# Output projection with seven block products instead of eight for the first 768 tokens

## The chip, the cores and the metric

The kernel runs on one core of a Trainium2 chip. The metric is the device time of one execution in microseconds (us). Three runs of the kernel before took 2946.74, 2948.99 and 2950.83 us; the median is 2948.99.

A core has five engines that run at their own pace and meet at semaphores: TensorE (PE, matmul; its weight loads are listed as PEld), VectorE (DVE), ScalarE (ACT), GpSimd (POOL) and SyncE (SP). SP here only issues DMAs; GpSimd and ScalarE issue DMAs too, beside their own work, and an engine does its instructions in the order in which they stand.

## What is computed

The reference is one layer of a decoder with two token mixers, a state space recurrence (S5) and gated linear attention (GLA). 1088 tokens go through it: 64 of eight short sequences (stored first) and 1024 of the prompt. What matters here is the end of the layer:

```python
merged = sigmoid(m_a) * a_out + sigmoid(m_b) * b_out
y = x + gate[:, None] * (merged @ w_out)          # w_out: 2048 x 2048
...
y_prompt = rms_norm(hp, final_norm_gain)          # the same for the samples
```

So `merged @ w_out` is a product of 1088 x 2048 by 2048 x 2048. After it come a gate per channel (for the samples per sequence and channel), the residual x, and a root mean square norm over the 2048 channels of each token.

## The kernel before

Channels lie on the 128 partitions and tokens along the free dimension, so an activation of 2048 channels is 16 tiles of [128, 1088]. A float32 operand is held in two parts, `hi` and `lo`, and `mm3` (lines 64 to 71) makes a product of them in three matmuls: hi with hi, hi with lo, lo with hi. The weights are split while they stream. `wsplit` (line 44) loads a [128, 512] quarter of a column tile on SP's queue into a raw buffer `wraw`, ScalarE rounds it to `whi` (line 54) and VectorE subtracts to get `wlo` (line 56). There are two raw buffers in the weight pool and, where a second pool is given, two more; `whi` and `wlo` have six buffers each.

The projection is `final` (lines 1058 to 1132). It goes over three token chunks, `FCH = [(0, 416), (416, 416), (832, 256)]`, and for each over 16 column tiles j and 16 k tiles, so 16 x 16 x 3 = 768 matmuls a chunk. In the first chunk the column tiles go in groups of six and three first, because the merged activations are loaded and split meanwhile:

```python
x = self.stage("mx")
nc.gpsimd.dma_start(x, self.mscr[k])
mg.append(self.split_act(x, True, nc.gpsimd if k % 3 == 1 else None))
```

`mscr` is the DRAM scratch into which `merge` (lines 1027 to 1055) writes the merged columns, one [128, 1088] tile per column tile. The 32 activation tiles of the pool `act` hold first the operands of the two merge products and then the 16 merged tiles in two parts.

For each finished column tile `ev` (line 1070) loads the residual on GpSimd's queue (line 1073), multiplies the sum in PSUM by the gate and adds the residual on VectorE (1081 to 1084), squares on ScalarE (1089), adds to the running sum of squares `acc` on VectorE (1090), and scales on ScalarE (1091). After 16 column tiles the root is taken (1126 to 1128), and y is multiplied by it and stored, two column tiles at a time (1130 to 1132), on VectorE and GpSimd:

```python
e, r = (nc.gpsimd, rc) if (i % 3 == 2 if last else i not in (0, 2)) else (V, rs)
e.tensor_tensor(ys[i], ys[i], r.unsqueeze(1).broadcast_to([P, 2, n]), mul)
```

The order on each engine is set when the kernel is built: a scheduler takes the instructions in the order in which the program writes them and lets an engine take a later one where, by its own model of the times, the earlier one is not ready or has no free buffer. On the chip each engine then keeps that order. Buffers of a pool with the same tag are used in rotation.

Of the kernel before, what the change touches and what calls it, by code (L numbers as in the profile page):

```python
# [26 lines left out]
FCH = [(0, 416), (416, 416), (832, 256)]  # L27
# [4 lines left out]
class Hybrid:  # L32
# [58 lines left out]
    def product_k(self, w, js, act, nk, evict):  # L91
        """Two or three column tiles side by side, in steps of 2 k tiles."""
# [9 lines left out]
        if shared:  # L102
            # opens a sum over the whole bank for the two that share it
# [25 lines left out]
    def rsqrt(self, out, v, tmp):  # L129
        """out = (v + eps) ** -0.5; v is read twice, tmp is a scratch tile."""  # L130
        nc = self.nc
        nc.scalar.activation(tmp, v, AF.Sqrt, bias=self.eps)
        nc.vector.reciprocal(out, tmp)
        self.newton(out, v, tmp)
# [9 lines left out]
    def setup(self):  # L144
# [13 lines left out]
        # four unit matrices of 32 rows above each other  # L158
# [24 lines left out]
    def ada_chunk(self, j, ps):  # L183
        """mod[:, 2j:2j+2, :]: 256 columns of silu(c) @ w_ada + b_ada, channels on partitions."""
# [12 lines left out]
    def ada_mm(self, ps, k0, raw, n):  # L197
        """Rows of w_ada against silu(c), four k tiles side by side in groups of 32 columns."""
# [5 lines left out]
    def ada_out(self, j, ps):  # L204
# [6 lines left out]
        # the four column groups together  # L211
# [3 lines left out]
    def norm_in(self):  # L215
        """1 / rms of the tokens, on all partitions"""
# [28 lines left out]
    def modulate(self, k):  # L245
        """h[k] in two parts."""
# [4 lines left out]
        # gain * (1 + scale)  # L251
# [4 lines left out]
        # prompt: h without the shift, then samples  # L256
# [14 lines left out]
    # The two halves of the partitions hold the real and imaginary parts of the 64 states of a group.  # L271
# [3 lines left out]
    def s5_setup(self):  # L275
# [10 lines left out]
        with ExitStack() as ctx:  # L286
# [21 lines left out]
            def exp(out, x, w):  # L308
                """exp(x) to the last bits: 2**k times a polynomial"""
# [23 lines left out]
            # sine and cosine: nearest quarter turn, rest below pi/4, polynomials  # L333
# [59 lines left out]
            # cf = (abar - 1) / lambda  # L393
# [29 lines left out]
    def s5_tables_a(self, u):  # L423
# [21 lines left out]
        def outer(out, pr, pi, n, x, y, op):  # L445
            """out[g, t, h] = pr[g, t] * x[g, h] (op) pi[g, t] * y[g, h]"""
# [12 lines left out]
    def s5_tables_b(self, u, tables):  # L459
# [21 lines left out]
        # powers of the rotation between chunks, by doubling  # L481
# [86 lines left out]
    def s5_run(self):  # L568
        """All of S5, in steps between other products."""
# [26 lines left out]
    def evict_u(self, j, c, t0, n, ps):  # L596
        """u in rows of [8 tokens of a chunk][136 chunks]"""
# [18 lines left out]
        # parts of ga: hi, lo, hi  # L616
# [32 lines left out]
    def evict_v(self, j0):  # L649
        """v with tokens on partitions: blocks of 128 tokens, the first of 64"""  # L650
        nc = self.nc

        def ev(j, c, t0, n, ps):
# [10 lines left out]
            if first:  # L664
                # the samples again in the layout of parts
# [17 lines left out]
    def gla_pool(self, ctx):  # L683
# [25 lines left out]
    def gla_load(self, hd, t0, n):  # L709
# [10 lines left out]
        if n == 64:  # L720
            # read as columns that nothing comes of
# [11 lines left out]
    def gla_run(self):  # L733
        """All of the GLA, in steps between other products."""
# [21 lines left out]
    def gla_unit(self, hd, t0, n, inputs, following):  # L756
        """head hd, tokens t0:t0+n; n = 256: two chunks of 128 of the prompt; n = 64: the samples"""
# [13 lines left out]
        # log gates (times 16) and their sums within the chunks  # L771
# [20 lines left out]
        # scores, [s, t], by halving: pairs across the middle of blocks of 2m tokens  # L792
        # in blocks of 32 tokens: scd[s, chunk, t of the same block]
# [16 lines left out]
        def decays(m):  # L810
            """queries and keys of the blocks, with the decays from and to the middle"""
# [41 lines left out]
        # decays from the start and to the end of the chunks  # L853
# [21 lines left out]
        if samp:  # L875
            # each row its part
# [79 lines left out]
    def ada_gates(self):  # L956
        """The last eight column chunks of the conditioning product, in steps between other products."""
# [11 lines left out]
    def split_act(self, x, on_act=False, engine=None):  # L969
        """The two parts of a [128, T] tile."""  # L970
# [87 lines left out]
    def final(self):  # L1058
# [5 lines left out]
        for t0, n in FCH:  # L1064
# [29 lines left out]
            for js in groups:  # L1094
# [12 lines left out]
                if start:  # L1107
                    self.p2ctx.close()
                    p3 = self.pool("p3")
# [176 lines left out]
```

## Time and profile before

| | |
|---|---|
| runs | 2946.74, 2948.99, 2950.83 us |
| profiled execution, span from first to last instruction | 2947.8 us |
| PE busy | 2890.1 us (98%) |
| DVE, ACT, POOL busy | 1344.5, 941.1, 263.4 us |
| output projection, first matmul to end of span | 2525.8 to 2947.8 us |
| granted TensorE clock, mean | 0.994 of 2.4 GHz |

The profile is of one execution; the page gives its span, and the median of the runs lies 1.2 us above it. Busy time is the time in which an engine had an instruction at work. Matmuls overlap in the engine, so the pace of a matmul is read from the distance of starts and not from its own duration. A view by windows gives for each stretch the busy time and the count of instructions of each engine, the granted clock, the share of time in which the DMA engines were busy, and what they moved.

### The profile page before, as it was taken

The numbers are of one execution on the slowest core, as the hardware profiler recorded it, in microseconds if no ns is written. First come the engines' busy times: TensorE is split into PE (matmuls) and PEld (weight loads), VectorE is DVE, ScalarE is ACT, GpSimd is POOL, SyncE is SP. The second block draws the span as 40 slices with busy tenths as digits, with TensorE's granted clock in tenths as the row PEclk, the third lists the DMA queues.
The fourth block names the chain that finished last, engine by engine and source line by source line (L and its number), as shares of the span: only waits on it lengthen the run. The fifth ranks groups of instructions, "written<-read, shape, count | busy, mean of one in ns | idle before, by whom it ended". The sixth has DMA issues, their size and how long they took to land.

```text
span 2947.8 us, 49487 instructions
## 1 busy us (share of the span) xinstructions
PE 2890.1 (98%) x19584; PEld 2762.2 (94%) x19584; DVE 1344.5 (46%) x3424; ACT 941.1 (32%) x1735; POOL 263.4 (9%) x430
## 2 busy tenths in 40 slices
PE   7999999999999999999999999999999999999988
PEld 3799999999989999999999999999999999899988
DVE  3587778751234444444453111114662233556455
ACT  4222222222234434443443111422232111444434
POOL 0002122210000000000000000301010000203021
PEclk9999999999999999999999999999999999999999
DMA  9634444442232222222223344423274333555455
GB/s 377 242 117 122 120 128 117 128 123 75 85 126 100 84 83 72 85 80 77 81 86 105 98 146 132 115 76 102 97 231 136 112 114 116 191 164 181 145 173 168
DMA packets 221881, 376.59 MB, mean 128 GB/s; under 512 B 35153, under 2 KB 111729, under 8 KB 219473
## 3 DMA queue, kind: packets, MB, share of 16 engines
q1 hardware_dynamic: 159856, 256.26, 26.8%
q0 software_dynamic: 24720, 75.59, 8.4%
q10 hardware_dynamic: 37072, 41.59, 4.1%
q8 instruction: 154, 2.52, 0.3%
q14 instruction: 79, 0.64, 0.1%
HBM read 288.44 MB, written 76.51 MB: 124 GB/s over the span
## 4 chain that ended last, share of the span: by engine, by line
PE 67%; DMA 2%; DVE 1%; ACT 1%; issue 1%; POOL 0%; DVEq 0%; ACTq 0%; POOLq 0%
PE mm L71 20%; PE mm L69 20%; PE mm L70 20%; DMA wraw<-in_w_out_dram 1%; DMA bz<-zbs 1%; PE bg L831 1%; PE bg L69 1%; PE bg L71 1%; PE bg L70 1%; PE bg L201 1%; PE bg L939 0%; PE bg L940 0%; PE bg L932 0%; DMA mx<-mscr 0%; DVE wlo L56 0%
## 5 line engine op out<-in xcount | busy, mean ns | idle before, releaser
L69 PE MATMUL mm<-hh,whi 128*128 128x384 f32 (+1 forms) x3360 | 1101.3, 329 | 4.2 <-ACT hh L264 4.2
L71 PE MATMUL mm<-hh,wlo 128*128 128x384 f32 (+2 forms) x3360 | 1103.0, 329 | 0.0
L70 PE MATMUL mm<-hl,whi 128*128 128x384 f32 (+1 forms) x3360 | 1100.0, 328 | 2.4 <-DVE hl L266 2.4
L56 DVE TENSOR_TENSOR wlo<-wraw,whi 128x512 fp32r<-128x512 f32 x560 | 406.1, 729 | 634.7 <-ACT whi L54 627.2
L69 PEld LDWEIGHTS mm<-hh,whi 128*128 128x128 f32 x3360 | 630.5, 188 | 19.2 <-issue 10.0
L70 PEld LDWEIGHTS mm<-hl,whi 128*128 128x128 f32 x3360 | 630.6, 188 | 10.1 <-DVE hl L266 3.6
L71 PEld LDWEIGHTS mm<-hh,wlo 128*128 128x128 f32 x3360 | 630.5, 188 | 5.5 <-issue 2.8
L54 ACT ACTIVATE whi<-wraw 128x512 fp32r<-128x512 f32 x560 | 351.3, 630 | 771.8 <-PE mm L70 561.6
L69 PE MATMUL mm<-ahi,whi 128*128 128x384 f32 (+3 forms) x1656 | 542.0, 328 | 13.4 <-DVE y L1084 10.4
L71 PE MATMUL mm<-ahi,wlo 128*128 128x384 f32 (+3 forms) x1656 | 542.2, 328 | 2.9 <-DVE wlo L56 2.9
L70 PE MATMUL mm<-alo,whi 128*128 128x384 f32 (+3 forms) x1656 | 541.6, 327 | 0.0
L69 PEld LDWEIGHTS mm<-ahi,whi 128*128 128x128 f32 x1656 | 313.5, 189 | 17.1 <-issue 11.0
L71 PEld LDWEIGHTS mm<-ahi,wlo 128*128 128x128 f32 x1656 | 313.5, 189 | 4.8 <-DVE wlo L56 3.5
L70 PEld LDWEIGHTS mm<-alo,whi 128*128 128x128 f32 x1656 | 313.6, 189 | 1.1
L635 ACT ACTIVATE ev<-mm 128x384 f32<-128x384 f32 (+1 forms) x120 | 55.9, 466 | 237.4 <-PE mm L71 234.4
L1042 DVE TENSOR_TENSOR m<-m,mm 128x384 f32<-128x384 f32 (+1 forms) x96 | 50.5, 529 | 146.9 <-PE mm L71 146.9
L645 DVE TENSOR_TENSOR ev<-ev,mm 128x384 f32<-128x384 f32 (+1 forms) x45 | 23.8, 530 | 181.3 <-ACT ev L644 181.2
L946 POOL TENSOR_TENSOR on<-on 128x256 f32<-128x256 f32 (+1 forms) x20 | 13.1, 653 | 961.3 <-ACT on L945 961.3
L644 ACT ACTIVATE ev<-mm 128x384 f32<-128x384 f32 (+1 forms) x45 | 21.1, 468 | 176.5 <-PE mm L71 176.3
L1040 ACT ACTIVATE m<-m 128x1088 f32<-128x1088 f32 x32 | 35.6, 1113 | 119.3 <-DMA m<-mbs 91.3
L480 POOL DMA_DIRECT2D tm<-kd x128 | 65.0, 516 | 43.0 <-DMA kd<-kk 18.8
L991 POOL DMA_DIRECT2D yt<-y x64 | 34.1, 540 | 380.1 <-ACT m L207 259.6
(334 smaller groups left out, 2580.6 us busy)
## 6 DMA issues: line engine op xcount, KB each, us to landing
wraw<-in_w_in_dram SPq DMA_DIRECT2D x288, 256.0 KB
wraw<-in_w_out_dram SPq DMA_DIRECT2D x192, 256.0 KB
adaraw<-in_w_ada_dram SPq DMA_DIRECT2D x64, 512.0 KB
gateraw<-in_w_ada_dram SPq DMA_DIRECT2D x16, 1024.0 KB
x<-in_xT_dram SPq DMA_DIRECT2D x16, 544.0 KB
m<-mas POOLq DMA_DIRECT2D x16, 544.0 KB, 4.9
m<-mbs POOLq DMA_DIRECT2D x16, 544.0 KB, 5.0
mscr<-m POOLq DMA_DIRECT2D x16, 544.0 KB, 3.1
```

Of the source, the lines that this page charges most:

```text
L54: nc.scalar.activation(hi, raw, AF.Copy)
L56: nc.vector.tensor_tensor(lo, raw, hi.bitcast(F32), ALU.subtract)
L69: nc.tensor.matmul(ps, hi[:, c], ah[:, sl], start=start, stop=False)
L70: nc.tensor.matmul(ps, hi[:, c], al[:, sl], start=False, stop=False)
L71: nc.tensor.matmul(ps, lo[:, c], ah[:, sl], start=False, stop=stop)
L201: self.nc.tensor.matmul(ps[i:i + 32, :256], self.c32[:, k, :], raw[:, (k - k0) * 256:(k - k0 + 1) * 256], start=k < 4, stop=k >= KT - 4, t ...
L480: nc.gpsimd.dma_start(tm[16 * s:16 * s + 16], kd[0:16, :, 16 * (7 - s):16 * (7 - s) + P])
L635: nc.scalar.activation(e[:, :n], ps[:, :n], AF.Copy, scale=scale)
L831: nc.tensor.matmul(o, gs, blk(gs, w)[:, :, m:w], start=True, stop=True, tile_position=(0, 32 * i))
L991: nc.gpsimd.dma_start(yv[r:r + 16], self.yscr[2 * i + uu][:, g, :].rearrange("(t h) c -> h t c", h=16))
L1040: nc.scalar.activation(st["m"], st["m"], AF.Sigmoid)
L1042: V.tensor_tensor(mm, mm, ps[:, :n], ALU.mult)
```

## The change

The first 768 tokens are cut into two halves of 384 (`SH`), the 16 k tiles into two halves of eight, and the 16 column tiles into eight pairs. In each pair the product is one of 2x2 blocks: weights a11, a12 (column tile j1, first and second half of k), a21, a22 (column tile j2) and merged activations 11, 12, 21, 22 (half of k, half of tokens). It is made with seven block products and sums of blocks on both sides (Winograd's form). The sums s1 to s4 are of weight blocks, t1 to t4 of activation blocks. Seven sweeps, one for each product, go over the eight pairs. The last 320 tokens (`FT`) are done plainly, four column tiles side by side and then one at a time.

`left` makes the weight operand of one product, a [128, 512] quarter block: it loads one or two blocks on SP's queue, adds or subtracts on GpSimd, and splits on ScalarE and VectorE. s1 and s2 are also stored to DRAM by GpSimd's queue, because later sweeps use them. `right` makes one k tile of the activation operand of the next sweep: it loads one to four halves on GpSimd's queue, takes up to three differences on GpSimd, and splits. Where in each sweep the finished sum in PSUM goes is written in `final`; `fin` adds the residual, and the sum of squares is now added on GpSimd. The output stays in 16 tiles `Y` of [128, 1088] in place of those that held half of the merged operands. The raw buffers in the second pool grow from two to eight. The root for the first 768 tokens is taken after the first four column tiles of the last part, and their y is multiplied and stored during the others, mostly on GpSimd. Comments and docstrings go as well.

```diff
-FCH = [(0, 416), (416, 416), (832, 256)]
+SH = 384
+FT = T - 2 * SH
...
-            raw = pool.tile([P, QK4], F32, tag="wraw", name="wraw3", bufs=2)
+            raw = pool.tile([P, QK4], F32, tag="wraw", name="wraw3", bufs=8)
...
+    SWEEPS = (("a11", "11"), ("a12", "21"), ("s1", "t1"), ("s2", "t2"), ("s3", "t3"), ("a22", "t4"), ("s4", "22"))
+
+    def left(self, w, an, pair, q, scr, raws):
...
+        def load(src):
+            raw = raws()
+            nc.sync.dma_start(raw, src)
+            return raw
+        blk = lambda j, k: load(w[j][:, (2 * k + q) * QK4:(2 * k + q + 1) * QK4])
+
+        def both(x, y, op):
+            nc.gpsimd.tensor_tensor(x, x, y, op)
+            return x
+        if an == "a11":
+            x = blk(j1, 0)
+        elif an == "a12":
+            x = blk(j1, 1)
+        elif an == "a22":
+            x = blk(j2, 1)
+        elif an == "s1":
+            x = both(blk(j2, 0), blk(j2, 1), ALU.add)
+            nc.gpsimd.dma_start(scr[0][:, q, :], x)
+        elif an == "s2":
+            x = both(load(scr[0][:, q, :]), blk(j1, 0), ALU.subtract)
+            nc.gpsimd.dma_start(scr[1][:, q, :], x)
+        elif an == "s3":
+            x = both(blk(j1, 0), blk(j2, 0), ALU.subtract)
+        else:
+            x = both(blk(j1, 1), load(scr[1][:, q, :]), ALU.subtract)
+        hi = self.wp.tile([P, QK4], F32R, tag="whi", name="whi", bufs=6)
+        nc.scalar.activation(hi, x, AF.Copy)
+        lo = self.wp.tile([P, QK4], F32R, tag="wlo", name="wlo", bufs=6)
+        nc.vector.tensor_tensor(lo, x, hi.bitcast(F32), ALU.subtract)
+        return hi, lo
+
+    def right(self, b, k, o, new):
...
+        sub = lambda out, x, y: nc.gpsimd.tensor_tensor(out, x, y, ALU.subtract)
+
+        def ld(i, h):
+            x = new()
+            nc.gpsimd.dma_start(x, self.mscr[8 * i + k][:, h * SH:(h + 1) * SH])
+            return x
+        if b in ("11", "21", "22"):
+            x = ld(int(b[0]) - 1, int(b[1]) - 1)
+        elif b == "t3":
+            x = ld(1, 1)
+            sub(x, x, ld(0, 1))
+        else:
+            x = ld(0, 1)
+            sub(x, x, ld(0, 0))
+            if b != "t1":
+                sub(x, ld(1, 1), x)
+            if b == "t4":
+                sub(x, x, ld(1, 0))
+        self.split_beside(o, x, SH)
...
+        def fin(j, h, c):
+            y, x = residual(j, h * SH, SH, c)
+            if acc[h] is None:
...
+            else:
+                nc.scalar.activation(x, y, AF.Square)
+                nc.gpsimd.tensor_tensor(acc[h], acc[h], x, add)
+            nc.scalar.activation(y, y, AF.Copy, scale=self.fgain[:, j:j + 1])
...
+        def raws():
+            self.nraw += 1
+            if p3 is None or self.nraw % 5 == 0:
+                return wraw()
+            return p3.tile([P, QK4], F32, tag="wraw", name="wraw3", bufs=8)
+        opx = lambda: self.stage("mx")[:, :SH] if p3 is None else p3.tile([P, SH], F32, tag="opx", name="opx", bufs=4)
+        for k in range(8):
+            self.right("11", k, sets[0][k], opx)
+        for r, (an, bn) in enumerate(self.SWEEPS):
+            B = sets[r % 2]
+            for i, pair in enumerate(pairs):
+                ps = self.psum(True)[:, :SH]
+                for q in range(2):
+                    hi, lo = self.left(w, an, pair, q, sscr[i], raws)
+                    for k in range(4):
+                        c = slice(k * P, (k + 1) * P)
+                        bh, bl = B[4 * q + k][:, :SH], B[4 * q + k][:, SH:2 * SH]
+                        nc.tensor.matmul(ps, hi[:, c], bh, start=q + k == 0, stop=False)
+                        nc.tensor.matmul(ps, hi[:, c], bl, start=False, stop=False)
+                        nc.tensor.matmul(ps, lo[:, c], bh, start=False, stop=q + k == 4 and k == 3)
+
+                if r < 6:
+                    self.right(self.SWEEPS[r + 1][1], i, sets[(r + 1) % 2][i], opx)
+                    if r == 0 and i == 7:
+                        self.p2ctx.close()
+                        p3 = self.pool("p3")
...
+                if r == 0:
+                    nc.scalar.activation(x, ps, AF.Copy)
+                elif r == 1:
+                    V.tensor_tensor(c11, x, ps, add)
+                    fin(pair[0], 0, c11)
+                elif r == 2:
+                    V.tensor_tensor(y, x, ps, add)
+                elif r == 3:
+                    V.tensor_tensor(x, x, ps, add)
+                    V.tensor_tensor(y, y, ps, add)
+                elif r == 4:
+                    V.tensor_tensor(x, x, ps, add)
+                    V.tensor_tensor(c22, y, ps, add)
+                    fin(pair[1], 1, c22)
+                elif r == 5:
+                    V.tensor_tensor(x, x, ps, sub)
+                    fin(pair[1], 0, x)
+                else:
+                    V.tensor_tensor(y, y, ps, add)
+                    fin(pair[0], 1, y)
+
+        n, t0 = FT, 2 * SH
...
+        for j0 in [0] + list(range(4, 16)):
+            js = range(0, 4) if j0 == 0 else [j0]
...
+            else:
+                for j in [j0 - 4] if j0 < 12 else [2 * j0 - 16, 2 * j0 - 15]:
+                    e = nc.gpsimd if j % 3 else V
+                    e.tensor_tensor(Y[j][:, :t0], Y[j][:, :t0], rs, mul)
+                    nc.gpsimd.dma_start(a["o_y"][j][:, :t0], Y[j][:, :t0])
...
+        for j in range(16):
+            e, r = (nc.gpsimd, rc) if j % 3 == 2 else (V, rs)
+            e.tensor_tensor(Y[j][:, t0:], Y[j][:, t0:], r, mul)
+            nc.sync.dma_start(a["o_y"][j][:, t0:], Y[j][:, t0:])
```

## Rows read from the trace of the kernel before

**Rows 1.** The page, part 1: busy time, share of the span, instructions

```profile
PE 2890.1 (98%) x19584; PEld 2762.2 (94%) x19584; DVE 1344.5 (46%) x3424; ACT 941.1 (32%) x1735; POOL 263.4 (9%) x430
```

**Rows 2.** Windows: stretch, length, busy time (instructions) by engine, clock, DMA share, GB/s

```profile
2525.80:2683.00 157.20, 153.68 (x802) 148.56 (x801) 81.53 (x139) 69.22 (x110) 18.28 (x23) 1.00 0.49 163
2683.00:2823.50 140.50, 140.50 (x740) 137.82 (x739) 74.69 (x97) 56.93 (x94) 26.02 (x25) 1.00 0.48 162
2823.50:2933.20 109.70, 97.18 (x771) 96.11 (x769) 69.39 (x97) 50.71 (x92) 26.00 (x26) 0.94 0.57 185
2600.00:2680.00 80.00, 80.00 (x426) 79.48 (x426) 38.98 (x79) 35.31 (x60) 4.83 (x9) 1.00 0.45 148
2890.00:2930.00 40.00, 40.00 (x335) 40.00 (x335) 23.12 (x39) 21.53 (x39) 2.69 (x5) 1.00 0.55 171
```

**Rows 3.** Timeline of PE: start, length, line; first of 24, 48 and 24 matmuls

```profile
2502.06 0.31 PE L69 MATMUL mm<-ahi,whi 128*128 128x320 f32 x1
...
2505.57 0.34 PE L69 MATMUL mm<-ahi,whi 128*128 128x384 f32 x1
...
2513.92 0.31 PE L69 MATMUL mm<-ahi,whi 128*128 128x320 f32 x1
```

**Rows 4.** Groups by line, 2520 to 2948: busy, mean ns, idle before, releaser

```profile
L56 DVE TENSOR_TENSOR wlo<-wraw,whi 128x512 fp32r<-128x512 f32 x188 | 147.3, 791 | 138.5 <-ACT whi L54 135.7 <-PE mm L70 1.1 <-PE mm L71 0.4
...
L54 ACT ACTIVATE whi<-wraw 128x512 fp32r<-128x512 f32 x188 | 117.3, 630 | 187.9 <-PE mm L70 131.7 <-DMA wraw<-in_w_out_dram 50.6 <-DVE rs L141 1.6
...
L1073 POOL DMA_DIRECT2D xr<-in_xT_dram x45 | 24.4, 541 | 293.4 <-DVE acc L1090 223.6 <-DVE y L1081 42.1 <-DVE y L1083 22.1
...
L1131 POOL TENSOR_TENSOR y<-y,rc 128x512 f32<-128x512 f32 x2 | 2.5, 1264 | 20.1 <-ACT rc L1124 20.1
```

**Rows 5.** Groups by line, the whole span, POOL alone

```profile
L946 POOL TENSOR_TENSOR on<-on 128x256 f32<-128x256 f32 x16 | 11.8, 736 | 652.2 <-ACT on L945 652.2
```

**Rows 6.** Timeline of POOL: start, length, line, count, idle time before

```profile
2512.51 2.65 POOL L977 TENSOR_TENSOR alo<-mx,ahi 128x1088 fp32r<-128x1088 f32 x1 [3.35 <-ACT ahi L974]
...
2691.38 15.06 POOL L1131 TENSOR_TENSOR y<-y,rs 128x832 f32<-128x832 f32 x6 [11.43 <-DVE rs L141]
```

**Rows 7.** Timeline of DVE

```profile
2502.75 0.69 DVE L56 TENSOR_TENSOR wlo<-wraw,whi 128x512 fp32r<-128x512 f32 x1
...
2512.98 2.73 DVE L56 TENSOR_TENSOR wlo<-wraw,whi 128x512 fp32r<-128x512 f32 x1 [0.23 <-ACT whi L54]
...
2699.72 0.64 DVE L1084 SCALAR_TENSOR_TENSOR y<-mm,mod,xr 128x416 f32<-128x416 f32 x1
2700.29 7.91 DVE L56 TENSOR_TENSOR wlo<-wraw,whi 128x512 fp32r<-128x512 f32 x5
```

**Rows 8.** The chain of waits from 2540: start, length, what was waited for

```profile
2547.06 0.64 ACT whi L54
...
2551.50 0.64 ACT whi L54
...
2556.61 0.64 ACT whi L54
```

**Rows 9.** Windows of dense or broken stretches, as in rows 2

```profile
2843.00:2848.00 5.00, 3.14 (x27) 2.94 (x25) 5.00 (x3) 0.63 (x1) 5.00 (x3) 1.00 0.46 170
2848.00:2852.00 4.00, 1.46 (x10) 1.25 (x10) 4.00 (x3) 0.00 (x0) 4.00 (x2) 0.89 0.25 87
2852.00:2857.00 5.00, 3.51 (x16) 3.54 (x17) 3.23 (x5) 2.10 (x5) 4.87 (x8) 0.50 0.70 230
2857.00:2862.00 5.00, 4.43 (x34) 4.23 (x32) 0.69 (x1) 0.49 (x1) 0.00 (x0) 0.90 1.02 359
...
2520.00:2540.00 20.00, 19.56 (x108) 18.98 (x106) 17.38 (x14) 10.92 (x12) 10.97 (x12) 1.00 0.90 315
```

**Rows 10.** DMA issues, 2520 to 2948: KB each, median us from issue to landing

```profile
xr<-in_xT_dram POOLq DMA_DIRECT2D x29, 208.0 KB, 3.5
```

More of the change, by code (lines that the diff above doesn't have):

```diff
@@ L1060, in final @@
         V = nc.vector
[L1061 to L1062 removed]
+        mul, add, sub = ALU.mult, ALU.add, ALU.subtract
         ev_tile = lambda name: self.ep.tile([P, 416], F32, tag="ev", name=name, bufs=3)
[L1064 to L1084 removed]
@@ new lines, in final, with residual @@
+        w = a["w_out"]
+        ops = [self.act(F32R, "op") for _ in range(16)]
+        Y = [self.act(F32, "y") for _ in range(16)]
+        sets = [ops[:8], ops[8:]]
+        pairs = [(j, j + 1) for j in range(0, 16, 2)]
+        sscr = [[self.dp.tile([P, 2, QK4], F32, name=f"ws{p}_{i}") for i in range(2)] for p in range(8)]
+        acc = [None, None]
+        def residual(j, t0, n, c, out=None):
+            x = ev_tile("xr")[:, :n]
+            nc.gpsimd.dma_start(x, a["xT"][j][:, t0:t0 + n])
+            p0 = 0
+            if t0 == 0:
+                p0 = TS
+                cv = c[:, :TS].rearrange("p (b t) -> p b t", t=8)
+                V.tensor_tensor(cv, cv, self.mod[:, 32 + j, 0:8].unsqueeze(2).broadcast_to([P, 8, 8]), mul)
+                V.tensor_tensor(c[:, :TS], c[:, :TS], x[:, :TS], add)
+            y = c if out is None else out
+            V.scalar_tensor_tensor(y[:, p0:], c[:, p0:], self.mod[:, 32 + j, 8:9], x[:, p0:], mul, add)
+            return y, x
@@ new lines, in final @@
+        n, t0 = FT, 2 * SH
+        mg = [(o[:, :n], o[:, n:2 * n]) for o in sets[1] + sets[0]]
+        facc = p3.tile([P, n], F32, tag="facc", name="facc")
+        for j0 in [0] + list(range(4, 16)):
+            js = range(0, 4) if j0 == 0 else [j0]
+            ps = [self.psum(True) for j in js]
+            for q in range(4):
+                if j0 == 0 and q == 2:
+                    for k in range(8):
+                        x = opx()[:, :n]
+                        nc.gpsimd.dma_start(x, self.mscr[8 + k][:, t0:])
+                        self.split_beside(sets[0][k], x, n)
+                wq = {j: self.wsplit(w[j][:, q * QK4:(q + 1) * QK4], pool=p3) for j in js}
+                for k in range(4 * q, 4 * q + 4):
+                    for i, j in enumerate(js):
+                        self.mm3(ps[i][:, :n], {q: wq[j]}, mg, k, slice(0, n), k == 0, k == KT - 1)
+            for i, j in enumerate(js):
+                y, x = residual(j, t0, n, ps[i][:, :n], Y[j][:, t0:])
@@ L1085, in ev @@
                 if j == 0:
-                    acc = p3.tile([P, 416], F32, tag="acc", name="acc")[:, :n]
-                    nc.scalar.activation(acc, y, AF.Square)
+                    nc.scalar.activation(facc, y, AF.Square)
                 else:
                     nc.scalar.activation(x, y, AF.Square)
-                    V.tensor_tensor(acc, acc, x, add)
+                    V.tensor_tensor(facc, facc, x, add)
                 nc.scalar.activation(y, y, AF.Copy, scale=self.fgain[:, j:j + 1])
-            groups = [range(0, 6), range(6, 9)] if first else []
@@ L1129, in final @@
-            for i in range(8):
-                e, r = (nc.gpsimd, rc) if (i % 3 == 2 if last else i not in (0, 2)) else (V, rs)
-                e.tensor_tensor(ys[i], ys[i], r.unsqueeze(1).broadcast_to([P, 2, n]), mul)
-                (nc.sync if last or i % 2 == 0 else nc.gpsimd).dma_start(a["o_y"][2 * i:2 * i + 2, :, sl].rearrange("j p t -> p j t"), ys[i])
+            if j0 == 0:
+                rs = p3.tile([P, 2 * SH], F32, tag="rs", name="rs")
+                for h in range(2):
+                    pm = self.psum(False)[:, :SH]
+                    nc.tensor.matmul(pm, self.ones_d, acc[h], start=True, stop=True)
+                    self.rsqrt(rs[:, h * SH:(h + 1) * SH], pm, ev_tile("rt3")[:, :SH])
+            else:
+                for j in [j0 - 4] if j0 < 12 else [2 * j0 - 16, 2 * j0 - 15]:
+                    e = nc.gpsimd if j % 3 else V
+                    e.tensor_tensor(Y[j][:, :t0], Y[j][:, :t0], rs, mul)
+                    nc.gpsimd.dma_start(a["o_y"][j][:, :t0], Y[j][:, :t0])
@@ new lines, in final @@
+        pm = self.psum(False)
+        tiles = [(0, P), (P, P), (2 * P, n - 2 * P)]
+        for i, (o, m) in enumerate(tiles):
+            nc.tensor.matmul(pm[:m, i:i + 1], facc[:, o:o + m], self.ones_d[:, 0:1], start=True, stop=True)
+        r = ev_tile("rs3")
+        V.memset(r[:, :3], 1.0)
+        for c, m in ((slice(0, 2), P), (slice(2, 3), n - 2 * P)):
+            self.rsqrt(r[:m, c], pm[:m, c], ev_tile("rt3")[:m, c])
+        rs = self.psum(False)[:, :n]
+        for i, (o, m) in enumerate(tiles):
+            nc.tensor.matmul(rs[:, o:o + m], r[:m, i:i + 1].broadcast_to([m, P]), self.ident[:m, :m], start=True, stop=True)
```

74 lines of the change are left out of this document (18 added, 56 removed).

## The prediction

> **What bounds the kernel now.** I read the page's busy shares first, then the stretch of the output projection in time windows, then the list of groups by line, the timelines of GpSimd and VectorE, and last the chain of waits.
>
> The page shows TensorE busy 98% and GpSimd 9% [rows 1]. Any product taken away is therefore worth its TensorE time, as long as the other engines keep up. In the windows the projection is a clean block: its first matmul starts at 2525.8 us, just after the last product of the merge, the first two token chunks end at 2823.5, the third at 2933.2, and the span at 2947.8 [rows 2]. The pace of a matmul is read from the same windows: 80.0 us / 426 = 0.188 us at 416 columns and 40.0 / 335 = 0.119 us at 256. At 384 and 320 columns it comes from the starts of neighbouring groups: 48 matmuls between 2505.57 and 2513.92 make 0.174 us, 24 between 2502.06 and 2505.57 make 0.146 us [rows 3]. The first two chunks hold 2 x 768 matmuls, 1536 x 0.188 = 289 us of the 297.7 they take; the third holds 768 x 0.119 = 92 us of 109.7. So before, TensorE sets the pace and loses 9 and 18 us. Where the 18 go is to be seen below: GpSimd's six multiplications stand across VectorE's weight splits, and TensorE is busy 63% and 37% beside them [rows 9].
>
> **What the change takes from TensorE.** Each sweep has 8 pairs of column tiles, each pair 2 x 4 x 3 = 24 matmuls of 384 columns: 24 x 0.174 = 4.18 us. Seven sweeps are 56 pairs, 234 us; the last 320 tokens are 768 x 0.146 = 112 us. That is 346 us against 381 at the same paces. The start gains too: the first sweep needs only halves of the first eight merged tiles, all stored long before, where the old start waited for sixteen full ones. If TensorE alone decided, the end would be 2525.8 + 234 + 112 + 16 (tail; 14.6 before, and now 16 single stores) = 2888 us.
>
> **What it adds on GpSimd.** All sums of weight blocks, the differences of merged halves, the running sums of squares, the loads of merged halves and of the residual, and the stores of weight sums stand on GpSimd's queue. Its prices: a DMA issue 0.54 us, an addition of 512 columns 1.26 us [rows 4]; an addition of 256 columns 0.74 [rows 5]. An addition of 384 has no row; it lies between 0.74 and 1.26, and I take the middle, 1.0. Per pair of column tiles, counted from `left`, `right` and `fin`:
> - sweep 1: 1 issue, 0.5 us
> - sweep 2: 3 issues, 2 additions of 384: 3.6
> - sweep 3: 5 issues, 2 of 512, 2 of 384: 7.2
> - sweep 4: 4 issues, 2 of 512, 1 of 384: 5.7
> - sweep 5: 5 issues, 2 of 512, 4 of 384: 9.2
> - sweep 6: 2 issues, 1 of 384: 2.1
> - sweep 7: 2 issues, 2 of 512, 1 of 384: 4.6
>
> TensorE needs 4.18 for the same pair. In sweeps 3, 4, 5 and 7 GpSimd is late, and TensorE waits for `whi` and `wlo` and, at each change of sweep, for the last right-hand block. The larger of the two in each sweep adds to 4.18 + 4.18 + 7.2 + 5.7 + 9.2 + 4.18 + 4.6 = 39.2 us, times 8 = 314 us for the 768 tokens. What GpSimd can do ahead is small: six `whi` and ten raw buffers hold about five pairs of weight sums, but sweep 2, in which they would be made, leaves GpSimd only 0.6 us per pair. The right-hand blocks cannot come early at all, since their tiles are read until one sweep before. So 308 is the low end.
>
> **What VectorE adds to that.** From 2691.38 GpSimd ran six multiplications of 832 columns in 15.06 us, 2.51 us each [rows 6]. By the two smaller sizes (0.74 and 1.26, so 2.05 ns a column) each should take 1.92. VectorE's weight split, 0.69 us when alone (0.79 in the mean of the projection [rows 4]), took 2.73 beside one of GpSimd's, and five of them took 7.91 us. An operation with one operand in PSUM ran in 0.64 in the midst of it, undisturbed [rows 7]. So operations of VectorE and GpSimd with both operands in SBUF exclude each other, and each one of VectorE that cuts in costs GpSimd 2.51 - 1.92, about 0.55 us. Per pair VectorE has three such operations (two weight splits, one split of the right-hand block), four where the residual, now read from SBUF, is added. If each cuts in, sweeps 2 to 5 and 7 become 4.7, 8.9, 7.3, 11.4 and 6.3. If none does, they stay. I take half, because GpSimd's DMA issues, some 40% of its time, let VectorE pass at no cost: 4.5, 8.0, 6.5, 10.3 and 5.4.
>
> The Trainium skill, page SBUF — State Buffer, section Who interferes with whom, says that a VectorE instruction with two SBUF inputs contends with a GpSimd instruction that reads SBUF, and that the first comer blocks the other for its whole length. The trace agrees on who blocks; by the whole 0.69 us in place of my 0.55, with every one cutting in, the end would be some 17 us past the upper bound given below.
>
> **The first sweep** has only the two old raw buffers, as the third pool opens at its end. The chain of waits shows what two give when nothing else holds them: split starts at 2547.06, 2551.50 and 2556.61, so 4.4 to 5.1 us for two quarters, which is one pair [rows 8]. I take 4.6, since six split quarters lie ready at its start.
>
> **The rest.** ScalarE has at most five instructions per pair, none wider than the weight split of 512 columns at 0.63 [rows 4]: 3.2 us at the most, under 4.18. The last 320 tokens have ten multiplications of 768 columns on GpSimd (1.75 us by the same slope) and 32 issues, in all some 40 us spread over 112, with six `wlo` to bridge a wait: I add 4 us. The bound from the other side is the 18 us that the old third chunk lost to six in a row.
>
> **The sum.** 8 x (4.6 + 4.5 + 8.0 + 6.5 + 10.3 + 4.2 + 5.4) = 348 us, less 8 for what is done ahead, = 340. 2525.8 + 340 + 112 + 4 + 16 = 2998 us, against 2947.8. Both are spans; the median of the runs shown lies 1.2 us above the span, less than I can tell, and I forecast 2998. The ends: 308 gives 2966; all cutting in, 8 x (4.6 + 4.7 + 8.9 + 7.3 + 11.4 + 4.2 + 6.3) = 379, gives 3037. The old time would be met at a sweep total of 2947.8 - 2525.8 - 132 = 290, which is 18 us below the low end.
>
> **TensorE's clock.** Between 2848 and 2857 the granted clock went from full (2.4 GHz) to 0.89 and then to half (1.2 GHz), after TensorE had been busy 63% and 37% of the time [rows 9]. In sweeps 3 to 5 it would be busy 52%, 64% and 41%. At the half level a pair takes 24 x 384 / 1.2 GHz = 7.7 us. This is hidden in sweeps 3 and 5 and costs up to 1.2 x 8 = 10 us in sweep 4; the end would be 3008, inside my range.
>
> **Rivals.**
> - GpSimd at its bare pace: VectorE's operations fall into its DMA issues. 2966 us. For it speaks that issues and additions alternate in `left`; against it that VectorE lost in every stretch where GpSimd was dense. Chance 0.15.
> - GpSimd waits for its own loads. In `right` a difference stands directly behind the load it needs, and a load from GpSimd lands 3.5 us after issue [rows 10]. Seven such differences per round of sweeps, 8 rounds, 3.5 us each would be 196 us if nothing were put between; the four staging buffers and other work in the order hide most. If a third stays, 65 us: 3063. This decides wherever the written order leaves no other work between load and difference. Chance 0.15.
> - The other side: the order of instructions lets GpSimd work evenly over all sweeps. Its sum is 33.0 x 8 = 264 us. Then the transfers decide: in sweeps 3, 4 and 5 a pair moves 2.16, 1.97 and 2.03 MB (weight blocks of 256 KB, merged halves of 192 KB, stores included). The queues moved 315 and 359 GB/s in their densest stretches [rows 9]; at 350 these are 6.2, 5.6 and 5.8 us, the other sweeps stay at 4.18, and 8 x 34.3 = 275 us ends at 2933, faster by 15. It needs GpSimd to be more than five pairs ahead, for which there are no buffers. Chance 0.10, of which 0.01 lies within 0.2%.
> - That the saving does not appear at all on TensorE can be excluded: the count of matmuls and their columns is fixed by the loops.
>
> **How the numbers follow.** The forecast has 0.55 (2975 to 3040), the bare pace 0.15 (2955 to 2975), the waiting loads 0.15 (beyond 3040), the faster side 0.10, and 0.05 is left for endings near the old time (0.03 within 0.2%, 0.02 above). About 0.2% (6 us) is what a measurement of this kernel can tell from no change. Faster 0.09; same 0.04; slower 0.87. The range 2955 to 3050 leaves out the faster side and the far half of the waiting loads.
>
> **What would show it.** Right: GpSimd busy near 70 to 90% in sweeps 3 to 5 and the weight split waiting for GpSimd's `wraw`; a sweep 5 of about 80 us and a sweep 6 of about 33; VectorE's splits at 1.5 us or more in sweep 5; a granted clock that drops there. Wrong: sweeps of even length near 34 us, GpSimd idle between its loads and its differences (the waiting loads), or DMA shares near 1.0 with GpSimd idle (the transfers).

## The result and the profile after

The changed kernel takes 3058.94 us (median of 4, 3057.35 to 3060.78) against 2947.86 of the kernel before in the same session. The ratio is 1.0373, 95% interval 1.0358 to 1.0387: slower by 111 us, where 50 were forecast. The profiled execution took 3059.61 us, its span is 3057.8. The direction was right, and so was the engine that sets the pace of the middle sweeps; the size was not, and the time lies 9 us above the range.

The page, part 1, of the changed kernel [rows 1 for before]: GpSimd went from 263 to 505 us, and TensorE has 188 matmuls less and yet the same busy time.

```profile
PE 2893.7 (95%) x19396; PEld 2757.9 (90%) x19396; DVE 1437.1 (47%) x3516; ACT 940.6 (31%) x1784; POOL 504.5 (16%) x728
```

The windows of the changed kernel, cut at the first matmul of each sweep, and then four stretches of the last 320 tokens (columns as in rows 2):

```profile
2525.10:2558.30 33.20, 33.20 (x193) 33.20 (x192) 13.88 (x21) 13.22 (x26) 3.72 (x7) 1.00 0.44 139
2558.30:2593.50 35.20, 34.36 (x194) 33.09 (x193) 28.41 (x36) 15.02 (x28) 21.23 (x25) 1.00 0.80 266
2593.50:2654.30 60.80, 41.49 (x195) 38.91 (x194) 49.16 (x48) 18.56 (x34) 48.60 (x59) 0.83 0.85 269
2654.30:2733.30 79.00, 44.98 (x193) 41.36 (x193) 32.12 (x42) 14.91 (x26) 62.10 (x77) 0.70 0.73 232
2733.30:2785.80 52.50, 39.90 (x195) 37.42 (x194) 32.17 (x36) 16.06 (x31) 40.70 (x45) 0.84 0.64 202
2785.80:2860.30 74.50, 44.21 (x193) 39.81 (x192) 37.35 (x62) 25.14 (x49) 52.43 (x66) 0.77 0.58 177
2860.30:2899.40 39.10, 35.88 (x195) 34.92 (x194) 38.40 (x49) 15.52 (x31) 29.21 (x32) 0.96 0.78 249
2899.40:2950.00 50.60, 49.90 (x333) 48.61 (x332) 38.63 (x59) 31.93 (x63) 18.98 (x25) 1.00 0.65 200
2950.00:2975.00 25.00, 12.21 (x72) 11.68 (x71) 24.14 (x15) 5.30 (x10) 23.54 (x12) 0.76 0.23 72
2975.00:3010.00 35.00, 30.16 (x182) 28.48 (x182) 13.95 (x24) 10.62 (x21) 10.41 (x20) 0.93 0.86 315
3010.00:3039.40 29.40, 29.40 (x191) 29.27 (x190) 14.00 (x27) 13.24 (x25) 2.69 (x5) 0.94 0.24 74
```

The first two sweeps run at TensorE's pace. Sweeps 3 to 6 take 60.8, 79.0, 52.5 and 74.5 us where TensorE alone would take 33.3 (measured below in a run without the waits), and GpSimd is busy 70 to 80% of them. Sweeps 3 to 7 hold 233 us of GpSimd work in 305.9 us. Then the last part loses time at one place: from 2950 to 2975 TensorE is busy half the time, GpSimd nearly all of it, and from 2975 the DMA queues are.

What one instruction cost in the sweeps, from the groups by line, 2525 to 2900, first GpSimd's:

```profile
L1077 POOL TENSOR_TENSOR wraw<-wraw,wraw 128x512 f32<-128x512 f32 x64 | 88.7, 1389 | 24.5 <-DMA wraw<-in_w_out_dram 13.2 <-DMA wraw<-ws 7.5 <-issue 1.8
L1104 POOL TENSOR_TENSOR opx<-opx 128x384 f32<-128x384 f32 x56 | 61.4, 1096 | 22.2 <-DMA opx<-mscr 21.4
L1108 POOL DMA_DIRECT2D opx<-mscr x96 | 52.6, 549 | 52.7 <-DVE op L1126 44.3 <-DVE y L1149 4.5 <-POOL opx L1104 2.1
```

and VectorE's split of a weight block:

```profile
L1098 DVE TENSOR_TENSOR wlo<-wraw,whi 128x512 fp32r<-128x512 f32 x107 | 130.2, 1233 | 32.1 <-ACT whi L1096 29.2 <-PE mm L1187 2.6
```

The prices of rows 4 held: 1.39 us for 1.26, 1.10 for the assumed 1.0, 0.55 for 0.54. VectorE's split went from 0.79 to 1.23 us in the mean: 1.79 in sweep 3, 1.31 in sweep 5. In the run with both sums early, where GpSimd is little used, it takes 0.72. That is the mark of the two engines shutting each other out.

Who waited, 2525 to 2900 (engine, line, whom for, us in all, times, longest):

```profile
ACT op L1125 <- POOL opx L1104: 113.7, 21, 12.7
...
PE mm L1185 <- ACT op L1125: 82.3, 17, 10.0
...
PE mm L1187 <- DVE wlo L1098: 11.8, 9, 3.4
```

TensorE waits for the right-hand operand `op`, that for ScalarE's rounding, and that for GpSimd's differences; the weight side is 12 us. And GpSimd's own waits in sweeps 3 to 6:

```profile
POOL opx L1108 <- DVE op L1126: 17.9, 11, 4.5
POOL opx L1104 <- DMA opx<-mscr: 16.4, 15, 2.8
POOL wraw L1077 <- DMA wraw<-in_w_out_dram: 13.2, 14, 2.2
POOL wraw L1077 <- DMA wraw<-ws: 5.5, 3, 2.3
```

That is 53 of the 63 us in which GpSimd was idle there: 18 before an issue, for a staging buffer (one of the four `opx` buffers into which merged halves are loaded) that the split has not yet freed; 16 before a difference, for the load issued just ahead; 19 before an addition, for weights. The split that frees a staging buffer runs on VectorE, so a part of the 18 may be VectorE's slowness; no run here separates it.

The last part, GpSimd's timeline of the changed kernel, beside the six multiplications of before [rows 6]:

```profile
2951.97 4.10 POOL L1255 TENSOR_TENSOR y<-y,rs 128x768 f32<-128x768 f32 x2 [0.88 <-DVE rs L142]
2956.02 0.58 POOL L1144 DMA_DIRECT2D xr<-in_xT_dram  x1
2956.62 18.61 POOL L1255 TENSOR_TENSOR y<-y,rs 128x768 f32<-128x768 f32 x8
2975.18 3.25 POOL L1256 DMA_DIRECT2D out_dram<-y  x6
```

VectorE's, in the same stretch: its own six multiplications take 15 us, and no weight split gets through meanwhile.

```profile
2954.29 15.02 DVE L1255 TENSOR_TENSOR y<-y,rs 128x768 f32<-128x768 f32 x6
2969.23 2.28 DVE L57 TENSOR_TENSOR wlo<-wraw,whi 128x512 fp32r<-128x512 f32 x1
```

Then all 16 stores leave within 18 us. The chain of waits shows what they do to the weight loads. In the chain of the kernel before, between 2542 and 2566, these took 2.9 to 4.4 us:

```profile
2542.57 4.39 DMA wraw<-in_w_out_dram
...
2562.38 2.85 DMA wraw<-in_w_out_dram
```

In the changed kernel they take up to 8.6:

```profile
2976.41 7.10 DMA wraw<-in_w_out_dram
...
2984.98 7.51 DMA wraw<-in_w_out_dram
...
2993.99 8.56 DMA wraw<-in_w_out_dram
```

### The profile page after: what moved, and what is told of

Same layout as the page of the kernel before. It is cut to its first block, busy times and chain, and to the rows that moved or that the text cites. A ratio compares the mean times of both kernels' runs of the same rounds, so it can differ in the third digit from the quotient of the medians.

```text
span 3057.8 us, 49726 instructions
## 1 busy us (share of the span) xinstructions
PE 2893.7 (95%) x19396; PEld 2757.9 (90%) x19396; DVE 1437.1 (47%) x3516; ACT 940.6 (31%) x1784; POOL 504.5 (16%) x728
## 4 chain that ended last, share of the span: by engine, by line
PE 60%; DMA 4%; DVE 4%; POOL 2%; issue 2%; ACT 1%; SPq 0%; DVEq 0%; POOLq 0%; ACTq 0%
PE mm L70 17%; PE mm L72 17%; PE mm L71 17%; DMA wraw<-in_w_out_dram 2%; DVE wlo L1098 2%; DMA opx<-mscr 1%; PE mm L1185 1%; PE mm L1187 1%; PE mm L1186 1%; POOL opx L1104 1%; PE bg L832 1%; DVE op L1126 1%; PE bg L202 1%; PE bg L940 0%; PE bg L941 0%
## 5 line engine op out<-in xcount | busy, mean ns | idle before, releaser
L55 ACT ACTIVATE whi<-wraw 128x512 fp32r<-128x512 f32 x432 | 269.9, 629 | 627.6 <-PE mm L71 420.6
L72 PE MATMUL mm<-ahi,wlo 128*128 128x384 f32 (+1 forms) x936 | 305.2, 326 | 0.0
L71 PE MATMUL mm<-alo,whi 128*128 128x384 f32 (+1 forms) x936 | 305.0, 326 | 0.0
L70 PE MATMUL mm<-ahi,whi 128*128 128x384 f32 (+1 forms) x936 | 304.1, 326 | 0.0
L1185 PE MATMUL mm<-op,whi 128*128 128x384 f32 x448 | 154.7, 369 | 82.4 <-ACT op L1125 82.3
L70 PEld LDWEIGHTS mm<-ahi,whi 128*128 128x128 f32 x936 | 175.5, 188 | 0.2 <-ACT ahi L975 0.2
L71 PEld LDWEIGHTS mm<-alo,whi 128*128 128x128 f32 x936 | 175.7, 188 | 0.0
L72 PEld LDWEIGHTS mm<-ahi,wlo 128*128 128x128 f32 x936 | 175.7, 188 | 0.0
L1187 PE MATMUL mm<-op,wlo 128*128 128x384 f32 x448 | 162.4, 363 | 12.0 <-DVE wlo L1098 11.8
L1185 PEld LDWEIGHTS mm<-op,whi 128*128 128x128 f32 x448 | 91.2, 209 | 90.2 <-ACT op L1125 89.2
L1186 PE MATMUL mm<-op,whi 128*128 128x384 f32 x448 | 162.9, 364 | 5.9 <-DVE op L1126 5.6
```

Of the source, the lines that this page charges most:

```text
L55: nc.scalar.activation(hi, raw, AF.Copy)
L70: nc.tensor.matmul(ps, hi[:, c], ah[:, sl], start=start, stop=False)
L71: nc.tensor.matmul(ps, hi[:, c], al[:, sl], start=False, stop=False)
L72: nc.tensor.matmul(ps, lo[:, c], ah[:, sl], start=False, stop=stop)
L1185: nc.tensor.matmul(ps, hi[:, c], bh, start=q + k == 0, stop=False)
L1186: nc.tensor.matmul(ps, hi[:, c], bl, start=False, stop=False)
```

## The experiments

Theory G: the sweeps are as long as GpSimd makes them, by its instructions and its waits in their order. Rivals: T, the transfers; C, the low TensorE clock; O, the order in which the blocks are written. Unless another base is named, each run changes the changed kernel (span 3057.8, sweeps 374.3 us in all, last part 140.0, tail 18.4; the tail goes from the last part's last matmul to the end of the span). A second figure in brackets is the seven sweeps together, from the first matmul of the first to the last of the seventh.

**Weight sums left out.**

```diff
         def both(x, y, op):
-            nc.gpsimd.tensor_tensor(x, x, y, op)
             return x
```

> Left out: the 64 additions and subtractions of weight blocks on GpSimd (the loads and stores around them stay). Theory G (GpSimd's own instructions and its waits in their order set the length of the middle sweeps): they take 88.7 us of GpSimd in the changed kernel, the sweeps shrink from 374 us to 290-305, the whole from 3059 to 2975-2990. Rival T (transfers set it): all bytes are the same, so 3050 or more. Rival C (the low TensorE clock sets it): no change of cause, 3040 or more.

Measured: 2999.91 us [319.4], 10 above the band but 59 below the changed kernel with the same bytes. Windows: the sweeps together, then sweep 6.

```profile
2523.00:2842.40 319.40, 260.44 (x1347) 251.19 (x1346) 175.09 (x291) 123.44 (x233) 182.17 (x254) 0.88 0.78 262
2735.90:2809.10 73.20, 46.02 (x194) 42.16 (x194) 38.27 (x64) 24.52 (x48) 53.95 (x73) 0.74 0.60 188
```

Rival T falls: the same bytes went through in 55 us less, at 262 GB/s over the sweeps, as much as in the busiest two before. Sweep 5 came down to 33.6 us, but sweep 6, which has no weight sum, stayed at 73.2 for 74.5. So 89 us less work bought 55, and something else holds sweep 6.

**Differences left out.**

```diff
-        sub = lambda out, x, y: nc.gpsimd.tensor_tensor(out, x, y, ALU.subtract)
+        sub = lambda out, x, y: None
```

> Left out: the differences of merged halves on GpSimd (56 instructions, 61.4 us); their loads stay. Theory G, and that TensorE waits above all for the right-hand operand: the sweeps shrink by 60-80 us, the whole to 2980-3000, and GpSimd no longer waits for its own loads to land. If only the weight side mattered: 3030 or more. Rival T: 3050 or more.

Measured: 2994.49 us [309.9], inside the band. Here 61 us less work bought 64. Sweep 6:

```profile
2745.10:2798.20 53.10, 41.23 (x195) 38.50 (x194) 30.55 (x50) 19.04 (x38) 31.10 (x43) 0.87 0.71 234
```

It is the t4 blocks, four loads and three differences each, that held sweep 6. The program writes them in sweep 5, but in the changed kernel GpSimd makes the last difference 53 us into sweep 6:

```profile
2838.32 1.00 POOL L1104 TENSOR_TENSOR opx<-opx 128x384 f32<-128x384 f32 x1
```

**Loads of merged halves on SP's queue.**

```diff
-            nc.gpsimd.dma_start(x, self.mscr[8 * i + k][:, h * SH:(h + 1) * SH])
+            nc.sync.dma_start(x, self.mscr[8 * i + k][:, h * SH:(h + 1) * SH])
```

> The 104 loads of merged halves are issued on SP's queue instead of GpSimd's; nothing is left out. Theory G: GpSimd loses 53 us of issues and the 18 us in which it stood before an issue for a staging buffer, the whole comes to 3000-3015. If the loads themselves are late (latency or bandwidth), 3045 or more. If SP's queue now stands for a staging buffer with weight loads behind it, slower than 3059.

Measured: 3006.62 us [322.0], inside the band, with nothing left out. By the trace it is 112 loads, not 104. An issue on GpSimd costs its 0.55 us and the wait that stands before it; SP bore both.

**Six staging buffers.**

```diff
-tag="opx", name="opx", bufs=4)
+tag="opx", name="opx", bufs=6)
```

> Six staging buffers for merged halves instead of four. GpSimd stood 18 us before an issue for a free staging buffer and 16 us before a difference for its load. If these waits are what makes the sweeps longer than GpSimd's work: 3025-3042. If they only fill time in which GpSimd would wait for something else: 3050-3062.

Measured: 3038.69 us [353.1], inside the band. GpSimd's waits in the same stretch of time, 2593 to 2860:

```profile
POOL opx L1108 <- DVE op L1126: 11.6, 7, 6.7
...
POOL opx L1104 <- DMA opx<-mscr: 4.3, 5, 1.5
```

These two went from 34 to 16 us, and the sweeps lost 21. So GpSimd's waits lie on the path as well as its work. The gain came in sweep 4 (73.0 for 79.0) and sweep 5 (36.6 for 52.5); sweep 6 stayed at 73.9.

**The right-hand block written first.**

```diff
                 ps = self.psum(True)[:, :SH]
+                if r < 6:
+                    self.right(self.SWEEPS[r + 1][1], i, sets[(r + 1) % 2][i], opx)
                 for q in range(2):
...
                 if r < 6:
-                    self.right(self.SWEEPS[r + 1][1], i, sets[(r + 1) % 2][i], opx)
```

> The changed kernel with the right-hand block of the next sweep written ahead of the pair's weight blocks instead of behind its matmuls. The same instructions, another order on each engine. Theory G in its strict form (GpSimd's 233 us of work in sweeps 3 to 7 set the length): within 15 us of 3059. Theory O (the right-hand blocks come late because they are written last, and TensorE stands for them 82 us): sweeps 4 and 6 shrink, the whole comes to 3020-3040.

Measured: 3057.5 us [378.0]. Sweeps 4 and 6, which were to shrink, took 86.4 and 75.1 us. The same work written in this order takes the same time; theory O falls.

**TensorE kept busier.** Eight matmuls more behind each quarter block of sweeps 3 to 6, of no use to the output.

```diff
+                    if 2 <= r <= 5:
+                        dm = self.psum(False)[:, :SH]
+                        for k in range(8):
+                            nc.tensor.matmul(dm, hi[:, k // 2 * P:(k // 2 + 1) * P], B[4 * q + k // 2][:, :SH], start=k == 0, stop=k == 7)
```

> The changed kernel with eight more matmuls of 384 columns behind each quarter block of sweeps 3 to 6, into a PSUM bank that nothing reads, so that TensorE stays busier. Rival C: TensorE's matmuls took 170 us instead of 133 in these four sweeps at the low clock; if those 37 us lie on the path, the granted clock rises and the sweeps shrink by 15 us or more. Theory G: TensorE waits anyway, and the sweeps stay within 8 us of 374 or grow.

Measured: 3078.77 us [383.3]. Windows of sweeps 3 to 6:

```profile
2599.70:2669.80 70.10, 59.31 (x322) 57.73 (x321) 50.02 (x49) 18.36 (x34) 58.17 (x71) 0.95 0.87 280
2669.80:2754.90 85.10, 63.03 (x323) 61.18 (x322) 33.08 (x42) 15.84 (x29) 62.69 (x75) 0.84 0.64 204
2754.90:2810.90 56.00, 55.71 (x322) 55.39 (x321) 42.94 (x50) 19.88 (x37) 45.41 (x57) 1.00 0.68 210
2810.90:2879.90 69.00, 61.13 (x321) 60.50 (x321) 30.21 (x50) 20.44 (x39) 45.21 (x54) 0.90 0.56 172
```

The granted clock rose from 0.83, 0.70, 0.84 and 0.77 to 0.95, 0.84, 1.00 and 0.90, and the four sweeps took 280 us for 267. The added matmuls are 512 x 0.174 = 89 us of work of their own, so this run bounds rival C and does not exclude it: sweep 6 became 5.5 us shorter, the other three longer. No gain is to be seen in the sum. The trace of the changed kernel narrows it further. At the start of sweep 4 (granted clock 0.50 from 2664 to 2684) the matmuls start 0.32 us apart, where they do so 0.174 apart at the full clock, and then TensorE waits 10 us (timeline of PE, 2654 to 2735):

```profile
2667.47 0.52 PE L1186 MATMUL mm<-op,whi 128*128 128x384 f32 x1
2667.79 0.52 PE L1187 MATMUL mm<-op,wlo 128*128 128x384 f32 x1
2678.26 1.33 PE L1185 MATMUL mm<-op,whi 128*128 128x384 f32 x3 [9.95 <-ACT op L1125]
```

A faster matmul before such a wait only lengthens the wait. Summed over sweeps 3 to 6, the distances of starts beyond 0.174 make 32 us, and an estimate from the same starts leaves at most 13 us of them that no following wait would have taken up. So, if the slower matmuls did not also delay GpSimd, the low clock cost at most 13 of the 134 us by which the four sweeps are longer than TensorE's own pace. The run with both sums early, below, fits: the waits are gone, and the clock is full.

**The paced end.** The scaling of the first 768 tokens moves into the last part and reads a copy of the gain made behind the sum of squares, so that each multiplication and store waits for its column tile.

```diff
-            nc.scalar.activation(y, y, AF.Copy, scale=self.fgain[:, j:j + 1])
 
         p3 = None
...
+                    fg = ev_tile("fg")[:, :1]
+                    nc.scalar.activation(fg, facc[:, :1], AF.Identity, scale=0.0, bias=self.fgain[:, j:j + 1])
+                    nc.scalar.activation(Y[j][:, :t0], Y[j][:, :t0], AF.Copy, scale=fg)
                     e = nc.gpsimd if j % 3 else V
```

> In the last part, the multiplication and store of the first 768 tokens of a column tile are made to wait for the column tile at which they are written (the scaling moves there and its scale is read behind the sum of squares), so they no longer come in one burst. Theory: the burst of ten multiplications (2952 to 2975) and of 16 stores (2975 to 2993) cost 22-26 us; the whole comes to 3033-3038 and the last part to 117-120 us. Rival (the last part is slow for want of raw buffers): 3055 or more.

Measured: 3050.97 us [382.7], 13 above the band. The last part is as expected, 117.7 us for 140.0:

```profile
2908.20:3025.90 117.70, 115.50 (x771) 114.50 (x770) 85.77 (x123) 70.28 (x137) 46.49 (x55) 0.99 0.62 197
```

But the sweeps took 8 us more and the tail 5. GpSimd multiplies and stores there until 3035.9, ten us past the last matmul; why the sweeps grew, with 32 instructions less on ScalarE in them, stays open (the order on the engines is another one).

**Weight sums made early.** All four sums are made while the products before the branches run, by a generator stepped between their parts; `left` loads one block each.

```diff
+    def presum(self, w):
...
+                A, B = ld(j2, 0), ld(j2, 1)
+                C, E = ld(j1, 0), ld(j1, 1)
+                yield
+                tt(B, A, B, ALU.add)
+                st(0, B)
+                tt(A, C, A, ALU.subtract)
+                st(2, A)
+                yield
+                tt(C, B, C, ALU.subtract)
+                st(1, C)
+                tt(E, E, C, ALU.subtract)
+                st(3, E)
+                yield
...
         self.gates = self.ada_gates()
+        self.steps = self.presum(a["w_out"])
```

> The sums s1 to s4 of weight blocks are made and stored during the products before the branches, where GpSimd has nothing to do; the sweeps load one block each. Nothing is left out. Theory G: the sweeps lose 89 us of GpSimd's additions and 18 us of its stores; against the run without the additions (sweeps 319 us) they come to 295-310, the whole to 2975-2992. Moving the work costs nothing where it goes (TensorE sets the pace there): the first sweep still starts at 2523-2529. Rival T: fewer bytes in the sweeps too, so this run alone does not tell it apart; the run without the additions does.

Measured: 2964.55 us [281.4], ratio to before 1.0055 (1.0034 to 1.0075); better than expected by 10 us, and sweep 6 is still 69.7 us: from 2590 to 2800 GpSimd still waits 28 us for its own loads and 21 for staging buffers. The first sweep starts at 2530.4, 5 us later than in the changed kernel and outside the 2523 to 2529 that was expected.

**Differences made early.** t1 to t4 are made when the upper eight merged tiles are evicted, from the tile at hand and the lower one loaded again; `right` loads one block.

```diff
+                    if j >= 8:
+                        s = lambda o, x, y: nc.gpsimd.tensor_tensor(o, x, y, ALU.subtract)
+                        lo, t = self.stage("tl")[:, :2 * SH], self.stage("tt")[:, :2 * SH]
+                        nc.gpsimd.dma_start(lo, self.mscr[j - 8][:, :2 * SH])
+                        s(lo[:, :SH], lo[:, SH:], lo[:, :SH])
+                        s(lo[:, SH:], mm[:, SH:2 * SH], lo[:, SH:])
+                        s(t[:, :SH], mm[:, SH:2 * SH], lo[:, :SH])
+                        s(t[:, SH:], t[:, :SH], mm[:, :SH])
+                        nc.gpsimd.dma_start(self.tscr[j - 8][:, 0, :], lo)
+                        nc.gpsimd.dma_start(self.tscr[j - 8][:, 1, :], t)
```

> The differences t1 to t4 of merged halves are made and stored while the last eight merged tiles are evicted; the sweeps load one block of 192 KB each. Nothing is left out. Theory G with the right-hand operand on TensorE's path: the sweeps lose 61 us of differences and 56 issues of 0.55 us, and come to 275-300 us; the whole to 2960-2985. If the weight side alone mattered: 3000 or more.

Measured: 2977.12 us [287.2], ratio 1.0097 (1.0077 to 1.0117), inside the band; sweep 6 is 33.3 us, sweeps 3, 4, 5 and 7, which have weight sums, 49.6, 41.8, 49.6 and 42.8. The first sweep starts at 2535.6, 10 us later than in the changed kernel.

**Both early.**

> Both sums made early. GpSimd has at most two issues and one addition per pair (2.1 us of TensorE's 4.18). Theory G: seven sweeps of 33.3 to 36 us, 235-250 together, the granted clock back at full, the last part as in the changed kernel (135-140): 2915-2932. Rival C (a clock that fell in the sweeps stays low): 2960 or more. Rival: VectorE, with up to 3.5 us per pair, becomes the bound: sweeps of 38 us or more where a residual is added.

Measured: 2924.49 us [236.2], ratio 0.9919 (0.9899 to 0.9938), inside the band. The third sweep and all seven:

```profile
2603.70:2637.00 33.30, 33.30 (x194) 33.30 (x194) 20.84 (x37) 14.83 (x27) 8.94 (x14) 1.00 0.61 195
2533.90:2770.10 236.20, 235.66 (x1344) 234.28 (x1345) 162.13 (x305) 132.30 (x248) 82.89 (x125) 0.99 0.66 213
```

This is TensorE's own 234 us of the prediction. The clock is full again without anything done for it. The sweeps start at 2533.9 instead of 2525.1, with one wait of 8.4 us in the first.

**Both early, end paced**, two column tiles in each of the first four steps.

```diff
-                for j in [j0 - 4] if j0 < 12 else [2 * j0 - 16, 2 * j0 - 15]:
+                for j in [2 * j0 - 8, 2 * j0 - 7] if j0 < 8 else [j0]:
```

> As the run with both made early, and the multiplications and stores of the last part paced as in the run with the paced end, but two column tiles in each of the first four steps so that the last step has one. Last part 117-120 us, tail 17-20: the whole 2893-2912, faster than both kernels by over 1%. If the late scaling takes back in the sweeps what it gives in the end (8 us in the run with the paced end): 2905-2915.

Measured: 2907.17 us (2906.03 to 2908.11), ratio 0.9861 (0.9845 to 0.9877), inside the band; sweeps 237.6, last part 113.9.

**The same, with the loads of merged halves on SP's queue** and a pool of two staging buffers for the first eight.

> The run with both sums early and the paced end, with the loads of merged halves on SP's queue and two staging buffers of their own for the first sweep's eight blocks, so that they no longer stand behind the last differences. The first sweep starts at 2524-2528 instead of 2534, the 8.4 us wait of TensorE in it is gone: 2895-2902.

Measured: 2903.59 us (2900.67 to 2911.64), ratio 0.9857 (0.9837 to 0.9877), 2 us above the band. The start is at 2524.6 and the 8.4 us wait is gone, but the second sweep takes 39.8 us for 35.5. It can't be told from the run before. What the moved work costs where it went, 1650 to 2050, changed kernel:

```profile
1650.00:2050.00 400.00, 400.00 (x2573) 386.63 (x2572) 84.42 (x141) 100.02 (x141) 34.71 (x65) 1.00 0.36 110
```

and this one:

```profile
1650.00:2050.00 400.00, 399.19 (x2564) 385.29 (x2563) 94.58 (x142) 100.02 (x142) 166.34 (x230) 1.00 0.57 182
```

132 us of GpSimd's work were added to this stretch, and TensorE's busy time fell by 0.8.

## Why the prediction was wrong

The span was forecast at 2998 and came to 3057.8, 60 us more. By terms: start -0.7, sweeps +34 (374 for 340), last part +24 (140 for 116), tail +2.

- **TensorE's saving, 24 matmuls of 0.174 us a pair and 112 us for the last part:** right. The runs with both sums early and the paced end show 33.3 us a sweep and 113.9.
- **GpSimd's prices and counts:** right. 8 x 28.8 = 230 us were counted for sweeps 3 to 7, 233 are there; over all seven, 264 and 258.
- **"What VectorE adds to that":** over-sized. Half of the cut-ins was to add 31 us to the sum. GpSimd's additions and differences grew by 64 x 0.125 + 56 x 0.10, about 13 us. The exclusion is there, but most of its cost fell on VectorE (0.79 to 1.23 us a split). The Trainium skill, page SBUF — State Buffer, section SBUF: two separate sides, says that the one that starts first holds the shared ports for its whole instruction and the other blocks. The trace agrees that they block; that VectorE was mostly the one that came second is read from the costs. The prediction also slips in its count here: sweeps 2 and 7 add the residual too, so by its own rule four operations cut in there, which puts 4 us more on the forecast and 13 on the upper end.
- **The first sweep:** put at 4.6 us a pair (36.8 us) for want of raw buffers; it took 33.2, TensorE's own pace.
- **GpSimd's waits in its own order:** the step that failed in the sweeps. The sum had no term for them; the rival "GpSimd waits for its own loads", given 0.15 and 65 us, was that term and belonged in the sum. Measured were 53 us of waits for staging buffers, loads and weights in sweeps 3 to 6. Six staging buffers took 18 of them away and 21 us of time; with the loads on SP's queue, GpSimd lost 53 us of issues and the waits before them, and the sweeps 52 us. So the bound was GpSimd's work plus these waits, and not the larger of GpSimd's work and TensorE's.
- **The share by sweep:** sweep 5 was to take some 82 us and sweep 6 some 33; they took 52.5 and 74.5. GpSimd falls behind within a sweep: it made 17 of the 24 differences of the t4 blocks in sweep 6, where TensorE waits for them. So what TensorE stood for was the right-hand block, 82 us, and not `whi` and `wlo`, 12 us. Leaving the differences out shrank sweep 6 to 53, making them early to 33.3; leaving out or moving the weight sums alone left it at 73 and 70.
- **"I add 4 us" for the last part:** the other step that failed. I had the 40 us of GpSimd "spread over 112", as the program writes them. But a multiplication depended on nothing but the root, and the order put all of them there: ten on GpSimd and six on VectorE within 23 us, 16 stores right behind. It cost 24 us, and pacing them gave 22 of these back. The prediction named the bound (the 18 us that six such multiplications had cost before) and did not use it.
- **The clock:** it fell, to 0.70 to 0.84, as [rows 9] had let expect. No run shows a cost of its own; the estimate from the starts of the matmuls leaves at most 13 us in sweeps 3 to 6. The 7.7 us a pair of the prediction agrees with the 0.32 us between starts there.
- **The faster side** was not met as it was put. GpSimd was not even over the sweeps, and no run was held by the transfers at the 350 GB/s of that rival. With both sums early the span ends at 2921, before its 2933, but for another reason: fewer bytes are left in the sweeps (213 GB/s), and TensorE sets the pace.

## What to carry to other kernels

An engine that shows 9% over the span can be the bound of a stage: count its instructions per step of that stage, and its queue's DMA issues and waits with them, before putting new work on it. Work that depends on early data only belongs where the engine is idle; the same sums, made before the sweeps, turned a loss of 3.7% into a gain of 0.8%, and pacing the end made it 1.4%. And a piece of work is spread over a stage only if something it depends on is; otherwise it comes in one burst as soon as it can.

## What was not expected of the hardware

- In the burst of stores the queues moved 315 GB/s over 35 us, and a store of 384 KB from GpSimd's queue took 8.6 us in the median to land. From the DMA issues from 2975 to 3010:

```profile
out_dram<-y POOLq DMA_DIRECT2D x16, 384.0 KB, 8.6
```

- Where VectorE and GpSimd shut each other out, the cost fell mostly on VectorE: 0.44 us more per split, against 0.1 us more per addition of GpSimd.
